# Mixture of softmaxes on one core: units in pairs through TensorE, and 4 MB stores

## The chip, the core and the metric

The kernel runs on one core of a Trainium2 chip. Its time is device time in microseconds from launch to end. The core's engines are TensorE (PE, matmuls into the accumulator memory PSUM), VectorE (DVE), ScalarE (ACT), GpSimd (POOL) and SyncE (SP), each with a queue of instructions worked off in order. 16 DMA engines move data between device memory and SBUF, the on-chip memory of 128 partitions; SP and ACT issue the DMAs here, and each has a queue of its own (q1 and q10 in the profile). A wait in an engine's queue holds everything behind it.

## What is computed

```
prior_probs = softmax(prior)                # (32, 128, 4): over the 4 heads
softmax     = softmax(logits)               # (32, 128, 4, 4096): over the vocabulary
out         = sum over the 4 heads of prior_probs * softmax   # (32, 128, 4096), fp32
```

268.4 MB of logits are read and 67.1 MB of output are written; a row of the vocabulary is 16 KB.

## The kernel before

The 4096 pairs of batch and position are cut into G = 32 groups of 128 rows, and each group into J = 2 units of M = 64 rows: N = 64 units. A unit's logits are 64 rows x 4 heads x 4096 values, 4 MB. They lie in one of SLOTS = 5 slots of 32 KB per partition: partition 2m + q holds heads 2q and 2q + 1 of row m, one behind the other (i = 0 and 1).

For each unit n and each i, `top` (L74) takes the negated maximum of 128 x 4096 values on DVE and then Exp on ACT, in place, with the sum in `dsum`. `weigh` (L83) takes the reciprocal on DVE, builds on POOL the 128 x 64 matrix `wt` (selection of the row, times 1/sum, times the prior's share) and issues eight matmuls of 512 columns: for c = 0 and 1, the column half c of the vocabulary goes to partitions 64c to 64c + 63 of the unit's accumulator. In the hardware each of these is two instructions, so that 16 stand in the profile for one pass. i = 0 starts the sums, i = 1 completes them. There are two accumulators of 128 x 2048 (four banks each), and a unit uses one of them, `accs[n % 2]`: unit n can be multiplied while unit n - 1 is evicted.

`evict` (L112) copies an accumulator on ACT to the group's home (L108): one half of `obuf`, `obuf[:, g % 2]`, so two groups alternate. As a partition holds only half of a row, `store` (L115) sends a group in two DMAs of 1 MB, each from 64 partitions, with 8 KB pieces. Both are issued on ACT's queue. The last groups are treated apart: units of groups 28 and 29 are put in slot 3, and stored after the loads (c = 0 on SP, c = 1 on ACT); groups 30 and 31 go out in parts as they are done.

The order of the work is written out by hand, and every engine keeps it. In turn n the kernel issues: `top(n, 0)`; `weigh(n - 1, 1)`, with the second pass of unit n - 1; on SP the load that reuses the slot of unit n - 1 (L165), which waits until PE has read it; `top(n, 1)`; `weigh(n, 0)`, with the first pass of unit n; `evict(n - 1)`; after every second unit the group's store.

Of the kernel before, what the change touches and what calls it, by code (L numbers as in the profile page):

```python
# [9 lines left out]
ALU = mybir.AluOpType  # L10
# [3 lines left out]
M = 64  # L14
J = 2
Q = 2
BANK = 512
SLOTS = 5


@with_exitstack
def kernel(
    ctx: ExitStack,
    tc: tile.TileContext,
    logits: bass.AP,
    prior: bass.AP,
    out: bass.AP,
):
    nc = tc.nc
    B, S, H, V = logits.shape  # L30
    R = M * J
    G = B * S // R
    N = G * J
    W = V // 2
    assert G * R == B * S and G == 32 and H == 2 * Q and V == 8 * BANK


    lg = logits.rearrange("b s h v -> (b s) h v").rearrange(
        "(g m j) (q i) v -> g j m q (i v)", m=M, j=J, i=Q
    )  # L40
    ov = out.rearrange("b s v -> (b s) v").rearrange("(g m j) v -> g m j v", m=M, j=J)
    pv = prior.rearrange("b s h -> (b s) h").rearrange("(g r) h -> g r h", r=R)

    cpool = ctx.enter_context(tc.tile_pool(name="cpool", bufs=1))
    psum = ctx.enter_context(tc.tile_pool(name="psum", bufs=1, space=bass.MemoryType.PSUM))

    slots = [cpool.tile([P, Q, V], FP32, name=f"slot{i}") for i in range(SLOTS)]

    obuf = cpool.tile([P, J, V], FP32, name="obuf")
    accs = [psum.tile([P, W], FP32, name=f"acc{i}") for i in range(2)]  # L50

    sel = cpool.tile([P, M], FP32, name="sel")
    wts = [[cpool.tile([P, M], FP32, name=f"wt{k}{i}") for i in range(Q)] for k in range(2)]
    pr = cpool.tile([G, R, H], FP32, name="pr")
    pn = cpool.tile([G, J, Q, M, Q], FP32, name="pn")
    pmax = cpool.tile([G, R], FP32, name="pmax")
    pp = cpool.tile([P, J, Q, G], FP32, name="pp")
    nmax = [cpool.tile([P, N], FP32, name=f"nmax{i}") for i in range(Q)]
    dsum = [cpool.tile([P, N], FP32, name=f"dsum{i}") for i in range(Q)]
    rden = [cpool.tile([P, N], FP32, name=f"rden{i}") for i in range(Q)]  # L60


    def slot(n):
        return slots[n % SLOTS if n < N - 6 else (4, 0, 1, 2)[(n - N + 6) % 4]]

    def load(n):
        src = lg[n // J, n % J]
        for i in range(0, Q, Q if n < N - 1 else 1):
            k = Q if n < N - 1 else 1
            nc.sync.dma_start(  # L70
                out=slot(n)[:, i : i + k], in_=src[:, :, i * V : (i + k) * V]
            )

    def top(n, i):  # L74
        x = slot(n)[:, i]
        nc.vector.tensor_reduce(  # L76
            out=nmax[i][:, n : n + 1], in_=x, axis=AX.X, op=ALU.max, negate=True
        )
        nc.scalar.activation(  # L79
            x, x, AF.Exp, bias=nmax[i][:, n : n + 1], accum_out=dsum[i][:, n : n + 1]  # L80
        )

    def weigh(n, i):  # L83
        nc.vector.reciprocal(rden[i][:, n : n + 1], dsum[i][:, n : n + 1])  # L84
        wt = wts[n % 2][i]
        nc.gpsimd.tensor_scalar(  # L86
            out=wt, in0=sel, scalar1=rden[i][:, n : n + 1],
            scalar2=pp[:, n % J, i, n // J : n // J + 1], op0=ALU.mult, op1=ALU.mult,
        )

        for b in range(W // BANK):
            for c in range(2):
                nc.tensor.matmul(  # L93
                    accs[n % 2][c * M : (c + 1) * M, b * BANK : (b + 1) * BANK],
                    lhsT=wt,
                    rhs=slot(n)[:, i, c * W + b * BANK : c * W + (b + 1) * BANK],
                    start=i == 0, stop=i == Q - 1,
                )

    def part(eng, g, c, js=slice(0, J), lo=0, hi=W):  # L100
        eng.dma_start(  # L101
            out=ov[g, :, js, c * W + lo : c * W + hi],
            in_=home(g)[c * M : (c + 1) * M, js, lo:hi],
        )

    HOLD = G - 4

    def home(g):  # L108
        x = slots[3] if HOLD <= g < G - 2 else obuf
        return x[:, g % 2].rearrange("p (j w) -> p j w", j=J)  # L110

    def evict(n, lo=0, hi=W):  # L112
        nc.scalar.copy(home(n // J)[:, n % J, lo:hi], accs[n % 2][:, lo:hi])  # L113

    def store(g):  # L115
        for c in range(2):
            part(nc.scalar, g, c)

    def prior_user(n):
        return max(k for k in range(n) if slot(k) is slot(n))  # L120

    with tc.manual_schedule():
        for n in range(SLOTS):
            load(n)
        nc.scalar.dma_start(out=pr, in_=pv)

        nc.gpsimd.memset(sel, 1.0)  # L127
        nc.gpsimd.affine_select(  # L128
            out=sel, in_=sel, compare_op=ALU.is_ge, fill=0.0, base=0,
            pattern=[[-Q, M]], channel_multiplier=1,  # L130
        )
        nc.gpsimd.affine_select(  # L132
            out=sel, in_=sel, compare_op=ALU.is_ge, fill=0.0, base=Q - 1,
            pattern=[[Q, M]], channel_multiplier=-1,
        )

        nc.vector.reduce_max(pmax, pr, axis=AX.X)  # L137
        nc.vector.tensor_sub(pr, pr, pmax.unsqueeze(2).to_broadcast([G, R, H]))  # L138
        nc.scalar.activation(pr, pr, AF.Exp)  # L139
        nc.vector.reduce_sum(pmax, pr, axis=AX.X)  # L140
        nc.vector.reciprocal(pmax, pmax)  # L141
        prv = pr.rearrange("g (m j) (q i) -> g j i m q", j=J, i=Q)
        pmv = pmax.rearrange("g (m j) -> g j m", j=J)
        for j in range(J):
            for i in range(Q):
                nc.vector.tensor_mul(  # L146
                    pn[:, j, i], prv[:, j, i], pmv[:, j].unsqueeze(2).to_broadcast([G, M, Q])
                )
        pq = pn.rearrange("g j i m q -> g j i (m q)")
        for t in range(P // 32):  # L150
            nc.vector.transpose(  # L151
                pp[32 * t : 32 * (t + 1)], pq[:, :, :, 32 * t : 32 * (t + 1)]
            )

        for n in range(N):
            w = n - 1
            top(n, 0)
            if n == N - 2:
                for g in (HOLD, HOLD + 1):
                    part(nc.scalar, g, 1)  # L160
            if w >= 0:
                weigh(w, 1)
                for k in range(SLOTS, N):
                    if prior_user(k) == w:
                        load(k)  # L165
                if w == N - 3:
                    for g in (HOLD, HOLD + 1):
                        part(nc.sync, g, 0)
            top(n, 1)
            weigh(n, 0)  # L170
            if w >= 0:
                evict(w)
                g = w // J
                if w % J == J - 1 and g < HOLD:
                    store(g)
                elif w == N - 3 or w == N - 2:
                    js = slice(0, J) if w == N - 3 else slice(0, 1)
                    part(nc.sync, g, 0, js)
                    part(nc.scalar, g, 1, js)

        n = N - 1
        weigh(n, 1)
        for lo in (0, W // 2):
            evict(n, lo, lo + W // 2)
            part(nc.sync, n // J, 0, slice(1, 2), lo, lo + W // 2)
            part(nc.scalar, n // J, 1, slice(1, 2), lo, lo + W // 2)
# [30 lines left out]
```

## Time and profile before

| | |
|---|---|
| median of three runs | 792.72 us (790.87 to 792.88) |
| the profiled execution: its time / its span | 793.28 / 791.6 us |
| busy: PE, DVE, ACT | 548.0, 573.3, 600.2 us (69%, 72%, 76%) |
| moved by DMA | 335.95 MB, mean 424 GB/s over the span |
| load of one unit | 4096 KB, 38.0 us from issue to landing (median) |
| store of half a group | 1024 KB, 21.5 us from issue to landing (median) |
| maximum / Exp / eviction, each | 4.41 / 3.71 / 1.82 us |

The time lies 1.7 us over the span, which runs from the first to the last instruction. Busy time is the sum of an engine's instructions. The time to landing of a DMA has its time in the queue in it. The page cuts the span into 40 slices and gives for each how busy an engine was, in tenths. A line number is a line of the kernel.

### The profile page before, as it was taken

Reading aid. Unit: us, or ns where it says so; the run is one execution under the profiler, and the core shown is the slowest. Engines: PE = TensorE matmul, PEld = TensorE weight load, DVE = VectorE, ACT = ScalarE, POOL = GpSimd, SP = SyncE. Lnnn points to the kernel's source line nnn. Section 1 sums busy time; section 2 is a strip of 40 time slices with the busy share of each in tenths; the row PEclk is TensorE's granted clock in tenths of the full one; section 3 lists DMA queues with packets and bytes.
Section 4 is the critical chain, followed back from the end, with each engine's and each line's share of the span. In section 5 each row is a group of like instructions: output and inputs, shape, how many; then the busy total and the mean of one; then the engine's idle time right before and its main releaser. Section 6 shows DMA issues by size and latency. Waiting matters only on the chain.

```text
span 791.6 us, 5426 instructions
## 1 busy us (share of the span) xinstructions
PE 548.0 (69%) x2048; PEld 160.4 (20%) x2048; DVE 573.3 (72%) x268; ACT 600.2 (76%) x323; POOL 51.6 (7%) x135
## 2 busy tenths in 40 slices
PE   0777568776687765767766767677578776687884
PEld 0222112221122221222211222222122221122221
DVE  5986867767768668677686676776867867768890
ACT  1897777787787787877877778778777787787894
POOL 0000000000000000000000000000000000000000
PEclk9999997899978899888999798789997799977897
DMA  9999999999999999999999999999999999999997
GB/s 376 442 416 431 431 428 430 432 431 427 434 432 435 429 432 436 430 433 431 434 429 433 431 431 429 428 435 431 429 431 432 431 432 433 433 430 436 429 416 229
DMA packets 18841, 335.95 MB, mean 424 GB/s; under 512 B 2144, under 2 KB 2144, under 8 KB 2432
## 3 DMA queue, kind: packets, MB, share of 16 engines
q1 hardware_dynamic: 10032, 272.63, 80.4%
q10 hardware_dynamic: 8784, 62.98, 19.1%
q8 instruction: 16, 0.26, 0.1%
q14 instruction: 9, 0.07, 0.0%
HBM read 268.50 MB, written 67.11 MB: 424 GB/s over the span
## 4 chain that ended last, share of the span: by engine, by line
DMA 73%; PE 12%; DVE 10%; ACT 2%; issue 1%; POOL 1%; ACTq 0%; SPq 0%; POOLq 0%
DMA slot<-in_logits_dram 73%; PE acc L93 12%; DVE nmax L76 10%; ACT slot L79 1%; POOL wt L86 1%; ACT obuf L113 1%; ACTq L101 0%; DVE rden L84 0%; SPq L70 0%; POOLq L86 0%; ACTq L79 0%; ACTq L113 0%
## 5 line engine op out<-in xcount | busy, mean ns | idle before, releaser
L93 PE MATMUL acc<-slot,wt 128*64 128x512 f32 x2048 | 548.0, 693 | 235.3 <-POOL wt L86 235.3
L76 DVE TENSOR_REDUCE nmax<-slot 128x1 f32<-128x4096 f32 x128 | 563.5, 4410 | 194.6 <-DMA slot<-in_logits_dram 194.6
L79 ACT ACTIVATE slot<-slot,nmax 128x4096 f32<-128x4096 f32 x128 | 474.6, 3708 | 178.0 <-DVE nmax L76 175.4
L93 PEld LDWEIGHTS acc<-slot,wt 128*64 128x64 f32 x2048 | 160.4, 158 | 622.0 <-POOL wt L86 311.8
L113 ACT COPY obuf<-acc 128x2048 f32<-128x2048 f32 (+1 forms) x61 | 110.9, 1817 | 4.8 <-PE acc L93 4.2
L86 POOL TENSOR_SCALAR wt<-sel,rden,pp 128x64 f32<-128x64 f32 x128 | 50.8, 397 | 725.7 <-DVE rden L84 721.8
L84 DVE RECIPROCAL rden<-dsum 128x1 f32<-128x1 f32 x128 | 19.6, 153 | 6.0 <-ACT slot L79 6.0
L79 ACT ACTIVATION_READ_ACCUMULATOR slot<-slot,nmax 128x1 f32 x128 | 23.9, 186 | 0.0
L113 ACT COPY slot<-acc 128x2048 f32<-128x2048 f32 x4 | 7.4, 1844 | 0.0
L137 DVE TENSOR_REDUCE pmax<-pr 32x128 f32<-32x512 f32 x1 | 0.7, 674 | 2.7 <-DMA pr<-in_prior_dram 2.7
L139 ACT ACT_TABLE_LOAD x1 | 1.3, 1283 | 1.2 <-PEq L201 1.2
L139 ACT ACTIVATE pr<-pr 32x512 f32<-32x512 f32 x1 | 0.6, 628 | 1.6 <-DVE pr L138 1.6
L151 DVE STREAM_TRANSPOSE pp<-pn 32x128 f32<-32x128 f32 x4 | 1.2, 302 | 0.1
L140 DVE TENSOR_REDUCE pmax<-pr 32x128 f32<-32x512 f32 x1 | 0.7, 674 | 0.7 <-ACT pr L139 0.7
L141 DVE RECIPROCAL pmax<-pmax 32x128 f32<-32x128 f32 x1 | 0.9, 942 | 0.0
L146 DVE TENSOR_TENSOR pn<-pr,pmax 32x128 f32<-32x128 f32 x4 | 0.9, 274 | 0.0
L138 DVE TENSOR_TENSOR pr<-pr,pmax 32x512 f32<-32x512 f32 x1 | 0.7, 678 | 0.0
L128 POOL TENSOR_SCALAR_AFFINE_SELECT sel<-sel 128x64 f32<-128x64 f32 x1 | 0.2, 241 | 0.1
L132 POOL TENSOR_SCALAR_AFFINE_SELECT sel<-sel 128x64 f32<-128x64 f32 x1 | 0.2, 240 | 0.1
L127 POOL MEMSET sel<- 128x64 f32 x1 | 0.2, 153 | 0.3 <-POOLq L201 0.3
L201 POOL MEMSET const-float32-0.0<- 128x1 f32 x1 | 0.1, 99 | 0.3 <-issue 0.3
L201 POOL MEMSET const-bfloat16-1.0<- 128x1 bf16 x1 | 0.1, 102 | 0.0
(2 smaller groups left out, 0.2 us busy)
## 6 DMA issues: line engine op xcount, KB each, us to landing
slot<-in_logits_dram SPq DMA_DIRECT2D x63, 4096.0 KB, 38.0
out_dram<-obuf ACTq DMA_DIRECT2D x57, 1024.0 KB, 21.5
slot<-in_logits_dram SPq DMA_DIRECT2D x2, 2048.0 KB, 20.2
out_dram<-slot SPq DMA_DIRECT2D x2, 1024.0 KB, 24.3
out_dram<-slot ACTq DMA_DIRECT2D x2, 1024.0 KB, 12.2
out_dram<-obuf SPq DMA_DIRECT2D x1, 1024.0 KB, 11.2
out_dram<-obuf SPq DMA_DIRECT2D x1, 512.0 KB, 4.3
out_dram<-obuf ACTq DMA_DIRECT2D x1, 512.0 KB, 6.2
```

The source lines that it names most:

```text
L76: nc.vector.tensor_reduce(out=nmax[i][:, n : n + 1], in_=x, axis=AX.X, op=ALU.max, negate=True)
L79: nc.scalar.activation(x, x, AF.Exp, bias=nmax[i][:, n : n + 1], accum_out=dsum[i][:, n : n + 1])
L84: nc.vector.reciprocal(rden[i][:, n : n + 1], dsum[i][:, n : n + 1])
L86: nc.gpsimd.tensor_scalar(out=wt, in0=sel, scalar1=rden[i][:, n : n + 1], scalar2=pp[:, n % J, i, n // J : n // J + 1], op0=ALU.mult, op1= ...
L93: nc.tensor.matmul(accs[n % 2][c * M : (c + 1) * M, b * BANK : (b + 1) * BANK], lhsT=wt, rhs=slot(n)[:, i, c * W + b * BANK : c * W + (b + ...
L113: nc.scalar.copy(home(n // J)[:, n % J, lo:hi], accs[n % 2][:, lo:hi])
L137: nc.vector.reduce_max(pmax, pr, axis=AX.X)
L138: nc.vector.tensor_sub(pr, pr, pmax.unsqueeze(2).to_broadcast([G, R, H]))
L139: nc.scalar.activation(pr, pr, AF.Exp)
L141: nc.vector.reciprocal(pmax, pmax)
L146: nc.vector.tensor_mul(pn[:, j, i], prv[:, j, i], pmv[:, j].unsqueeze(2).to_broadcast([G, M, Q]))
L151: nc.vector.transpose(pp[32 * t : 32 * (t + 1)], pq[:, :, :, 32 * t : 32 * (t + 1)])
```

## The change

Units are now taken through TensorE in pairs. Units 2k and 2k + 1 are the same half j of two neighbouring groups (`place`). In `pair_pass` the first one's rows go to partitions 0 to 63 and the second one's to partitions 64 to 127, each with its own weights, over the whole vocabulary: 16 matmuls (32 instructions) for one i, into both accumulators. A partition now holds a whole output row in the two accumulators. `pair_evict` copies both to `obuf[:, k % 2]`, and after two pairs a partition of `obuf` holds two neighbouring rows of the output, 32 KB in one piece. One DMA of 4 MB from all 128 partitions stores them: 32 KB pieces, on ACT's queue, after the eviction of every odd pair.

Units 0 to 55 are 28 pairs. The last eight units go singly, as before, with their results in slot 4 (groups 28 and 29) and in the slot of unit 60 (groups 30 and 31). The store of the last two pairs is issued on SP, behind the last load. The slots of a pair are reloaded together (`reload`), after the pair's second pass. The core of the diff:

```diff
+    TAIL = N - 8
+    def place(n):
+        if n < TAIL:
+            return 2 * (n // 4) + n % 2, n % 4 // 2
+        return n // J, n % J
     def slot(n):
-        return slots[n % SLOTS if n < N - 6 else (4, 0, 1, 2)[(n - N + 6) % 4]]
+        return slots[n % SLOTS if n < N - 5 else (n - N + 5) % 4]
...
+    def reload(n):
+        for k in range(SLOTS, N):
+            if max(x for x in range(k) if slot(x) is slot(k)) == n:
+                load(k)
...
+    def matmul(n, i, dst, lo):
+        nc.tensor.matmul(
+            dst, lhsT=wts[n % 2][i], rhs=slot(n)[:, i, lo : lo + BANK],
+            start=i == 0, stop=i == Q - 1,
+        )
+    def pair_pass(k, i):
+        for b in range(V // BANK):
+            for c in range(2):
+                acc = accs[b // 4][c * M : (c + 1) * M, b % 4 * BANK : (b % 4 + 1) * BANK]
+                matmul(2 * k + c, i, acc, b * BANK)
+    def pair_evict(k):
+        for h in range(2):
+            nc.scalar.copy(obuf[:, k % J, h * W : (h + 1) * W], accs[h])
+    def store(eng, k):
+        eng.dma_start(
+            out=ov[2 * k : 2 * k + 2].rearrange("g m j v -> (g m) j v"), in_=obuf
+        )
...
-    HOLD = G - 4
     def home(g):
-        x = slots[3] if HOLD <= g < G - 2 else obuf
+        x = slots[4] if g < G - 2 else slot(N - 4)
...
-        for n in range(N):
+        K = TAIL // 2
+        for k in range(K):
+            u, v = 2 * k, 2 * k + 1
+            top(u, 0)
+            if k:
+                weight(u - 1, 1)
+                pair_pass(k - 1, 1)
+                reload(u - 2)
+                reload(u - 1)
+            top(u, 1)
+            weight(u, 0)
+            if k:
+                pair_evict(k - 1)
+                if k % 2 == 0:
+                    store(nc.scalar, k // 2 - 1)
+            top(v, 0)
+            weight(u, 1)
+            top(v, 1)
+            weight(v, 0)
+            pair_pass(k, 0)
+
+        for n in range(TAIL, N):
...
+            if w == N - 3:
+                store(nc.sync, K // 2 - 1)
+                for g in (G - 4, G - 3):
+                    part(nc.sync, g, 0)
```

`weight` is the first half of the old `weigh`, without the matmuls; `unit_pass` is its second half, unchanged. In the loop over the last units `weight` and `unit_pass` stand where `weigh` stood, and in its first turn the second pass and the eviction of the last pair.

## The prediction

> **What bounds the kernel now.** I read the page first: slices, queues, chain, DMA issues.
>
> ```profile
> DMA  9999999999999999999999999999999999999997
> ...
> q1 hardware_dynamic: 10032, 272.63, 80.4%
> q10 hardware_dynamic: 8784, 62.98, 19.1%
> ...
> DMA 73%; PE 12%; DVE 10%; ACT 2%; issue 1%; POOL 1%; ACTq 0%; SPq 0%; POOLq 0%
> ...
> L113 ACT COPY obuf<-acc 128x2048 f32<-128x2048 f32 (+1 forms) x61 | 110.9, 1817 | 4.8 <-PE acc L93 4.2
> ```
>
> The 16 DMA engines are full from start to end, loads on q1 and stores on q10. The busiest engine, ACT, is at 76%. The evictions (L113) idled 4.8 us in all, and none of that for a store. To see what a load and a store cost, the timeline of DVE at the start, where no store runs yet:
>
> ```profile
> 23.29 4.42 DVE L76 TENSOR_REDUCE nmax<-slot 128x1 f32<-128x4096 f32 x1 [0.89 <-DMA slot<-in_logits_dram]
> 33.00 4.42 DVE L76 TENSOR_REDUCE nmax<-slot 128x1 f32<-128x4096 f32 x1 [0.84 <-DMA slot<-in_logits_dram]
> 42.71 4.42 DVE L76 TENSOR_REDUCE nmax<-slot 128x1 f32<-128x4096 f32 x1 [0.84 <-DMA slot<-in_logits_dram]
> ```
>
> A 4 MB load takes 9.71 us (432 GB/s). The timeline of PE much later shows the rhythm with stores:
>
> ```profile
> 607.14 8.78 PE L93 MATMUL acc<-slot,wt 128*64 128x512 f32 x32 [2.10 <-POOL wt L86]
> 619.25 9.85 PE L93 MATMUL acc<-slot,wt 128*64 128x512 f32 x32 [3.33 <-POOL wt L86]
> 631.36 8.78 PE L93 MATMUL acc<-slot,wt 128*64 128x512 f32 x32 [2.26 <-POOL wt L86]
> 643.47 3.65 PE L93 MATMUL acc<-slot,wt 128*64 128x512 f32 x16 [3.33 <-POOL wt L86]
> 647.86 3.65 PE L93 MATMUL acc<-slot,wt 128*64 128x512 f32 x16 [0.73 <-POOL wt L86]
> ```
>
> One unit each 12.11 us, so its 1 MB of stores costs 12.11 - 9.71 = 2.40 us. That is the load's rate already (9.71 / 4 = 2.43).
>
> **Larger store packets: 0 us.** Four units cost 4 x 12.11 = 48.4 us now, and 5 x 9.71 = 48.6 us as four loads and one 4 MB store. Loads and stores already move at one rate, so 32 KB packets have nothing to win. Bounds: by the whole-run queue shares q10's 62.98 MB took 2419 us of engine time (19.1% of 16 x 791.6) and would take 2352 at q1's rate, so at most 67 / 16 = 4 us are gained; the other way, 13 times 48.6 - 48.4, some 2 us are lost.
>
> **How the queues share.** The DMA view of 300 to 400 us, then that of the first store (issued at 47.42 into full load traffic):
>
> ```profile
> q1 hardware_dynamic: 1180, 34.47, 79.8%
> q10 hardware_dynamic: 1182, 8.63, 20.5%
> ```
>
> ```profile
> out_dram<-obuf ACTq DMA_DIRECT2D x1, 1024.0 KB, 17.5
> ```
>
> Packets of the two queues come one for one. A load packet is 32 KB, a store packet 8 KB now: stores get a fifth of the bytes and are spread evenly. With 32 KB packets a store takes half of the traffic while it lasts. The first store had 8 packets per engine, each beside one load packet: 8 x (9.71 + 2.40) / 8 = 12.1 us, so 17.5 - 12.1 = 5.4 us went before its first byte and after its last. The new 4 MB store has 8 packets per engine of a load packet's size: 2 x 9.71 + 5.4 = **24.8 us** from issue to landing. Bounds: with the fixed part of the 64 KB prior load on idle queues (1.9 us in all) 21.3; with a store that stands behind two whole queued loads, 44.
>
> [...]
>
> **What waits for that store.** Before, two groups' outputs alternate in obuf's halves. Now both halves are filled by two pairs and leave in one DMA, and the next pair_evict writes half 0: it must wait for the landing. On ACT the order is fixed: behind that eviction stands the Exp of the pair's second unit, behind it (by its sum) DVE's reciprocal, the POOL weight and both passes of the pair, and behind these the next eviction, the next store and, on SP, the reload of two slots at once.
>
> [...]
>
> **The loop, from one store issue to the next (four units):**
> - store to landing: 24.8
> - two evictions of 128x2048: 1.84 + 1.82 = 3.7 (ACT rows)
> - Exp with its accumulator read: 3.71 + 0.19 = 3.9
> - reciprocal, POOL weight, start of PE: 0.84 (773.61 to 774.45 in the timeline)
> - two pair passes of 32 matmuls: PE has idled about 11 us by then. After a gap 32 matmuls took 8.57 to 10.09 us, without one 2 x 3.55. I take 9.3 + 7.1 = 16.4; bounds 14.2 (both without a loss) and 20.2 (both at 10.09)
> - the last eviction half, then the issue: 1.9
>
> Sum **51.5 us**, against 48.6 that DMA needs: the loop is the bound, and the queues run dry for about 3 us each time round (from the last load of the five slots to the late reload). The other half of the loop is covered: from a store's issue over its 0.57 us on ACT, one Exp, 0.84, 16.4 and 1.9 the pair ends after 23.6 us, under the 28.5 of landing and evictions. DVE (573 us in all) and the reloads of the first pair end earlier too.
>
> **Start.** Units 0 to 4 land at 13.6, 23.3, 33.0, 42.7, 52.4. Pair 0's passes start at 33.0 and end at 49.4; its eviction at 51.3; Exp of unit 3 at 55.2; pair 1's passes at 56.0 to 72.4; the first store is issued at 74.3. The two reloads at 72.4 come about 2 us after the queue ran dry (unit 6 lands at 71.8, a load starts 1.5 us after its release).
>
> **End.** The 13th store is issued 12 loops later: 74.3 + 12 x 51.5 = 692.3. From there to the end of pair 27's passes 24.8 + 3.7 + 3.9 + 0.8 + 16.4 = 49.6, one eviction 1.9; then ACT has units 57 to 63 with 7 x 7.6 for Exp, 6 x 1.85 for evictions and 1.8 for issues: 66.1; then before's own end after the last Exp, 777.2 to 791.6 = 14.4. Together 132.0. The 4 MB of the last pair store, now behind the loads on SP, and 8 MB of parts take 29 us beside it: hidden. Span 692.3 + 132.0 = 824.3. The profiled execution took 793.28 for a span of 791.6, so 1.7 lie around it: **826 us**, against 793.28 (the median, 792.72, is 0.6 lower).
>
> The rest costs nothing: the new order of the units and the map of slots at the end change no size; matmuls, weight loads, Exp and reductions keep number and shape; 42 DMA issues less on ACT (0.57 each) give 24 us to an engine that then waits.
>
> **Rivals.**
> - **The store lands in time: faster.** If it lands within 21.5 us, the loop falls to about 48.2, below DMA's 48.6. For it: the prior load's 1.9 us. Against: the 17.5. Then 52.4 + 2 + (59 loads + 13 stores) x 9.71 = 753.5 to the last load, 12.6 MB at 432 GB/s 29, some 4 for the small parts and the landing: 786.5, so 788 us: the late stores fill an end in which the slice now has 229 GB/s. Deciding point: 21.9 us from issue to landing. Chance 0.13.
> - **Half of it.** Passes and landing near their lower ends, loop 48.7 to 49.8: 790 to 804 us. Chance 0.11.
> - **The columns no longer overlap**, because the two tiles now hold different weights and stream different slots: 32 matmuls take twice 7.1. Both halves of the loop grow to 37, the time to above 1100. Against: each matmul already has its own weight load (2048 of each). Chance 0.02. **The store stands behind queued loads** (44 us): loop 71, about 1070. Chance 0.04.
> - Forecast, loop 49.8 to 53: 804 to 845. Chance 0.70.
>
> **Numbers.** A microsecond in the loop is 12 to 13 in the time, hence the width: 792 to 846 leaves out the fast case, the far ones and little else (0.2). A measurement here can tell about 0.3% from no change: 790.3 to 795.1. The fast case lies below it (0.13); of "half of it" 0.04 lies in it; slower 0.83.
>
> **What would show it.** Right: ACT copies that idle some 6 to 7 us at every second pair with a DMA of out_dram as releaser, stores of 4096 KB landing 24 to 25 us after issue, DMA near 406 GB/s in the middle, equal packet counts while a store runs, PE bursts of 64 matmuls with 7 and 11 us between them. Wrong: copies that wait only for PE, slices at 430 GB/s, stores landing under 22 us, or 32 matmuls at 14 us.

## The result and the profile after

The changed kernel takes 833.98 us (median of four runs, 831.83 to 834.74) beside 792.8 of the kernel before: 1.0521 times as long [1.05, 1.0543]. The profiled execution took 834.57, with a span of 832.8. The forecast was 826, in a range of 792 to 846. One of the six executions of e7 (below) took 1916.78 us and is left out of e7's figures.

The GB/s row of the page of before, with 40 slices of the span:

```profile
GB/s 376 442 416 431 431 428 430 432 431 427 434 432 435 429 432 436 430 433 431 434 429 433 431 431 429 428 435 431 429 431 432 431 432 433 433 430 436 429 416 229
```

The page of the changed kernel: slices, queues, the group of the evictions, the stores.

```profile
DMA  9999999999999999999999999999999999999996
GB/s 381 428 427 379 434 396 403 429 386 443 383 428 427 376 430 380 422 428 384 430 380 444 430 381 429 369 435 433 373 430 378 430 408 401 430 379 427 413 342 230
...
q1 hardware_dynamic: 10176, 276.83, 80.2%
q10 hardware_dynamic: 2592, 58.79, 16.7%
...
L126 ACT COPY obuf<-acc 128x2048 f32<-128x2048 f32 x56 | 103.2, 1866 | 139.9 <-DMA out_dram<-obuf 104.1
...
out_dram<-obuf ACTq DMA_DIRECT2D x13, 4096.0 KB, 25.1
...
out_dram<-obuf SPq DMA_DIRECT2D x1, 4096.0 KB, 41.5
```

Read the DMA row and the row under it together. The tenths still say 9 everywhere. The GB/s row shows the loss: it swings between some 370 and 440, where before stays near 430, and the mean over the span is 403 where before had 424. The store's larger packets are there (q10 fell from 8784 to 2592 packets). The evictions, which idled 4.8 us in all before, now idle 139.9, and 104.1 of that for a store.

Where that wait stands is seen on ACT, in one loop from store issue to store issue. The columns are start, duration, engine, line, operation, and in brackets the idle time and its releaser:

```profile
73.71 0.37 ACTq L129 DMA_DIRECT2D out_dram<-obuf  x1
...
90.54 0.19 ACT L92 ACTIVATION_READ_ACCUMULATOR slot<-slot,nmax 128x1 f32 x1
99.22 3.63 ACT L126 COPY obuf<-acc 128x2048 f32<-128x2048 f32 x2 [8.49 <-DMA out_dram<-obuf]
102.73 3.72 ACT L92 ACTIVATE slot<-slot,nmax 128x4096 f32<-128x4096 f32 x1
...
123.56 1.86 ACT L126 COPY obuf<-acc 128x2048 f32<-128x2048 f32 x1 [1.57 <-PE acc L105]
125.46 0.34 ACTq L129 DMA_DIRECT2D out_dram<-obuf  x1
```

and on PE beside it:

```profile
101.18 1.94 PE L105 MATMUL acc<-slot,wt 128*64 128x512 f32 x2 [5.59 <-issue]
107.36 16.17 PE L105 MATMUL acc<-slot,wt 128*64 128x512 f32 x64 [4.24 <-POOL wt L99]
```

At 90.73 ACT has nothing left that it may do: next in its order are the copies, and they overwrite what the store of 73.71 still reads. They start at 99.22, 25.5 us after that store's issue. Exp and its accumulator read end at 106.54, the 64 matmuls run from 107.36 to 123.53, the last copy ends at 125.42, and the next store goes out. 25.5 + 3.5 + 3.8 + 0.8 + 16.2 + 1.9 is the loop of 51.7 us. Its mean over the twelve from 73.71 to 689.24 is 51.29.

The end, as windows (busy time of PE, PEld, DVE, ACT and POOL with their instructions, then granted clock, DMA share, GB/s):

```profile
780.00:800.00 20.00, 15.28 (x68) 4.23 (x64) 18.33 (x9) 18.55 (x11) 1.57 (x4) 1.00 1.00 390
800.00:810.00 10.00, 8.66 (x32) 2.55 (x32) 0.33 (x2) 5.94 (x5) 0.79 (x2) 0.83 0.99 305
810.00:820.00 10.00, 0.11 (x2) 0.00 (x0) 0.00 (x0) 2.02 (x2) 0.00 (x0) 0.75 1.01 376
820.00:832.80 12.80, 0.00 (x0) 0.00 (x0) 0.00 (x0) 0.00 (x0) 0.00 (x0) 0.50 0.46 137
```

The last load lands at 793.8 and the last Exp ends at 804.2, so that from 800 on little is left to compute and only stores are under way. The DMA engines show as full until 820, yet move 305 and 376 GB/s instead of the 432 of the loads.

### The profile page after: what moved, and what is told of

Read it like the earlier page. It is cut to its first block, busy times and chain, and to the rows that moved or that the text cites. A ratio compares the mean times of both kernels' runs of the same rounds, so it can differ in the third digit from the quotient of the medians.

```text
span 832.8 us, 5348 instructions
## 1 busy us (share of the span) xinstructions
PE 544.7 (65%) x2048; PEld 162.4 (20%) x2048; DVE 572.2 (69%) x268; ACT 600.2 (72%) x323; POOL 51.2 (6%) x135
## 3 DMA queue, kind: packets, MB, share of 16 engines
q10 hardware_dynamic: 2592, 58.79, 16.7%
## 5 line engine op out<-in xcount | busy, mean ns | idle before, releaser
L105 PE MATMUL acc<-slot,wt 128*64 128x512 f32 x2048 | 544.7, 675 | 265.4 <-POOL wt L99 196.1
L105 PEld LDWEIGHTS acc<-slot,wt 128*64 128x64 f32 x2048 | 162.4, 155 | 646.8 <-issue 402.7
L126 ACT COPY obuf<-acc 128x2048 f32<-128x2048 f32 x56 | 103.2, 1866 | 139.9 <-DMA out_dram<-obuf 104.1
L144 ACT COPY slot<-acc 128x2048 f32<-128x2048 f32 (+1 forms) x9 | 15.0, 1663 | 6.9 <-PE acc L105 4.2
## 6 DMA issues: line engine op xcount, KB each, us to landing
out_dram<-obuf ACTq DMA_DIRECT2D x13, 4096.0 KB, 25.1
out_dram<-obuf SPq DMA_DIRECT2D x1, 4096.0 KB, 41.5
out_dram<-slot ACTq DMA_DIRECT2D x1, 512.0 KB, 19.7
```

Of the source, the lines that this page charges most:

```text
L105: nc.tensor.matmul(dst, lhsT=wts[n % 2][i], rhs=slot(n)[:, i, lo : lo + BANK], start=i == 0, stop=i == Q - 1,)
L126: nc.scalar.copy(obuf[:, k % J, h * W : (h + 1) * W], accs[h])
```

## The experiments

The theories, with the letters used here. **S**: the eviction's wait for the store closes a loop (landing, eviction, Exp, passes, eviction, store) that is longer than the DMA work of four units. **P**: the pairing itself sets the pace. **Q**: a store that takes half of the traffic starves the loads. For the end, **W**: a late issue waits until an earlier DMA has landed (the ACT issue at 813.29 went out when the 41.5 us store had landed at 813.2); the expectations take it to be the DMA eight issues before. **N**: stores that read 64 partitions are slow when no loads run beside them.

### e1: smaller packets for the same store

`obuf`'s rows are set 64 bytes apart, so that its two rows no longer form one piece: 16 KB packets.

```diff
-    obuf = cpool.tile([P, J, V], FP32, name="obuf")
+    obuf = cpool.tile([P, J, V + 16], FP32, name="obuf")[:, :, :V]
```

> obuf's two rows stand 64 bytes apart, so the one 4 MB store goes out in 16 KB packets instead of 32 KB ones; nothing else changes. Theory S (the eviction that waits for the store's landing closes a loop through Exp, both passes, the next eviction and the next store): 16 store packets per engine, each beside a load packet, 16 x (1.214 + 0.607) + 5.4 = 34.5 us to landing instead of 25; the loop goes from the measured 51.3 to about 61, the time to about 950. Rival P (the pairing itself, with both accumulators taken and slots released by twos, sets the pace, and the store's wait is beside it): 834, no change. Rival Q (a store that takes half of the traffic starves the loads, and the time is lost there): it now takes a third, so faster, 805 to 820.

One run: 949.44 us.

```profile
L126 ACT COPY obuf<-acc 128x2048 f32<-128x2048 f32 x56 | 103.2, 1867 | 252.2 <-DMA out_dram<-obuf 217.8
...
out_dram<-obuf ACTq DMA_DIRECT2D x13, 4096.0 KB, 33.8
```

Landing goes from 25.1 to 33.8 us, 8.7 more; twelve loops of that are 104, and the time grew by 115. The loop itself went from 51.29 to 60.27 us, where some 61 were expected. A store that takes a smaller share of the traffic makes the kernel slower, which is the reverse of Q, and P knows nothing of packets. S holds.

### e2: the store cut in two

Each half of `obuf` has a DMA of its own (16 KB packets); the two are issued one behind the other, where the one was.

```diff
-        eng.dma_start(
-            out=ov[2 * k : 2 * k + 2].rearrange("g m j v -> (g m) j v"), in_=obuf
-        )
+        for j in range(J):
+            eng.dma_start(
+                out=ov[2 * k : 2 * k + 2, :, j].rearrange("g m v -> (g m) v"),
+                in_=obuf[:, j],
+            )
```

> The 4 MB store is issued at the same place as two DMAs of 2 MB, one for each half of obuf, so that the next pair's eviction waits for the first one's landing only. Bytes, packets (16 KB) and place are those of the padded kernel. Theory S: the first half lands after 8 x (1.214 + 0.607) + 5.4 = 20 us, the loop would be 46.5, under the 48.6 that DMA needs: 73.7 + 12 x 48.6 + an end of 143 + 1.7, about 801. Rival P: 834. Rival Q: the same as the padded kernel, 805 to 820 by its own count, since the traffic is the same.

799.64 us, 1.0097 times before [1.0079, 1.0114].

```profile
L126 ACT COPY obuf<-acc 128x2048 f32<-128x2048 f32 x56 | 102.9, 1860 | 30.6 <-PE acc L105 30.3
...
out_dram<-obuf ACTq DMA_DIRECT2D x26, 2048.0 KB, 24.4
```

The 24.4 is a median over both halves: the first ones land some 18.6 us after their issue (20 were expected), the second ones after some 30. A first half also goes out 2 to 4 us ahead of the second, while the copies into the second half still run, as the pair before has filled it. So it is free before the next copy asks for it, and no copy waits for a store. The loop takes 48.42 us, what DMA needs. The window of 300 to 600 us of before, of the changed kernel and of e2, in this order (the last figure is GB/s):

```profile
300.00:600.00 300.00, 209.95 (x780) 61.71 (x782) 219.21 (x100) 229.58 (x123) 19.83 (x50) 0.87 1.00 431
300.00:600.00 300.00, 201.35 (x736) 59.45 (x736) 208.30 (x96) 221.36 (x119) 18.48 (x47) 0.78 0.98 409
300.00:600.00 300.00, 210.40 (x804) 63.42 (x802) 221.15 (x99) 228.84 (x122) 19.26 (x49) 0.83 1.00 431
```

The rate is before's again. So 34.3 of the 41.2 us are the wait. The pairs, their order and the two slots reloaded at once are all still there.

### e3 and e10: an Exp ahead of the waiting eviction

In e3 `top(v, 0)` goes ahead of `pair_evict` in every turn; in e10 only for odd k, where the copies wait.

```diff
             weight(u, 0)
+            top(v, 0)
             if k:
...
-            top(v, 0)
```

> Maximum and Exp of the pair's second unit (first half) stand ahead of the previous pair's eviction instead of behind it; stores as in the changed kernel. Theory S: Exp, reciprocal and POOL leave the loop (4.7 us), 51.3 - 4.7 = 46.6, under DMA's 48.6: about 801, with stores that land 25 us after issue as now. Rival P: 834, as the pairs and the slots are handled as they were. Rival Q: 834, as the packets are the same.

e3: 809.0 us, 1.0204 times before [1.0166, 1.0242]. The copies wait 36.7 us for stores instead of 104.1, and the loop has 49.75 us instead of 51.29. The direction is S's, but 8 us of the expected gain are missing.

> Exp ahead of the eviction only in the pairs whose eviction waits for a store (odd k); in the others the eviction stays ahead, as in the changed kernel. Theory S with the reading of the run that moved Exp everywhere (there the other eviction, and so the next store, came to stand behind an Exp whose load was late): loop 25 + 1.9 + 16.4 + 1.9 = 45, under DMA's 48.6, about 798 to 802. If that reading is wrong: 806 to 811 again.

e10: 812.18 us, 1.0256 times before [1.0219, 1.0294]. A miss: my reading of e3 was wrong.

```profile
L126 ACT COPY obuf<-acc 128x2048 f32<-128x2048 f32 x56 | 101.9, 1854 | 4.3 <-PE acc L105 4.2
```

```profile
300.00:600.00 300.00, 203.93 (x776) 75.24 (x777) 213.31 (x97) 226.70 (x122) 18.87 (x48) 0.81 1.00 424
```

Now no copy waits for a store at all, and still the loops alternate between some 47.4 and 51.6 us, 49.58 in the mean, with the DMA engines full at 424 GB/s. The packet records show where it is: from 130 to 640 us a 32 KB load packet takes 1237 ns in the mean (1213 to 1215 in before and e2), and the slow ones come where the load queue is just running dry, because two slots are reloaded late and together (issues at 367.7 and 368.4). The store's larger packets are not needed for it: e1, with 16 KB store packets, has 1265 ns, and e4 (below), with no pair stores at all, 1256. Why a load packet is slow there no run takes apart; in e2 the two slots are reloaded together as well and nothing is lost. This part of e3 and e10 stays open.

### e4: no pair stores

The fourteen 4 MB stores are left out, everything else stays.

> The 14 stores of the pairs are left out (units 0 to 55 don't reach the output); evictions stay. Theory S: the pairs run at the rate of their own chain, Exp 3.9 + 0.84 + both passes 16.4 + the last eviction half 1.9 = 23.0 per pair, 46 per four units (loads alone need 38.8): 73.7 + 12 x 46 + an end of some 130, 755 to 765. Rival P (pairing alone costs the 51): 815 to 834. Rival Q (only the traffic counts): 38.8 per four units, some 665 to 690.

One run: 743.8 us. PE's timeline:

```profile
100.74 16.93 PE L105 MATMUL acc<-slot,wt 128*64 128x512 f32 x64 [6.47 <-POOL wt L99]
124.13 15.48 PE L105 MATMUL acc<-slot,wt 128*64 128x512 f32 x64 [6.47 <-POOL wt L99]
146.08 16.45 PE L105 MATMUL acc<-slot,wt 128*64 128x512 f32 x64 [6.47 <-POOL wt L99]
```

A pair every 22.75 us, 45.5 for four units. That is the pairing's own pace, and here it is the bound: the loads of four units need 38.8. It lies below the 48.4 us of four units with their stores, so P does not set the time of the changed kernel, with 3 us to spare in a loop. e4 is 11 us faster than S's lower end and some 13 under its sum: 6 of that are the twelve loops (45.5 against 46), and some 7 the end, which I had taken as 130 and which took 122.7.

### e5, e6 and e9: the end

In e5 the last unit is evicted and stored in one piece (two DMAs fewer, for W). In e6 and e9 each of the six 1 MB stores of groups 28 to 30 reads 128 partitions instead of 64, with as many bytes; e6 writes them as whole stretches, e9 to exactly the addresses of the changed kernel. In both the values of these three groups land in other places of the output than they should.

```diff
-        for lo in (0, W // 2):
-            evict(n, lo, lo + W // 2)
-            part(nc.sync, n // J, 0, slice(1, 2), lo, lo + W // 2)
-            part(nc.scalar, n // J, 1, slice(1, 2), lo, lo + W // 2)
+        evict(n)
+        part(nc.sync, n // J, 0, slice(1, 2))
+        part(nc.scalar, n // J, 1, slice(1, 2))
```

and in e9:

```diff
+        if js == slice(0, J):
+            rows = ov[g].rearrange("m j v -> (m j) v")
+            eng.dma_start(out=rows[:, c * W : (c + 1) * W], in_=home(g)[:, c])
+            return
```

> The changed kernel with the last unit's eviction and stores in one piece instead of two column halves: two DMAs less at the end. It asks why the end (from the 13th store's issue) took 143.6 us where 132.0 were forecast. Theory W (a DMA's issue waits until the DMA eight issues before it has landed, as the last four issues do in the trace, up to 822.8 us): the last issue comes at about 817, the time falls by 4 to 6 us, to 828 to 830. Theory N (with no loads beside them, stores from 64 partitions move at 300 to 390 GB/s instead of 432): bytes and shapes are the same, 832 to 834.

> The changed kernel with the six DMAs of 1 MB of groups 28, 29 and 30 reading all 128 partitions (half of each partition's bytes, 8 KB packets) instead of 64 partitions each: number, size, packets and places of issue stay; the rows of these three groups land in other places of the output. Theory N: 6.3 MB go at about 432 instead of some 345 GB/s, 3 to 5 us less, 829 to 831. Theory W: the waits stay, at most 1 us less, 833 to 834.

> As the run that took the six DMAs of 1 MB of groups 28 to 30 from 128 partitions, but each writes exactly the addresses that the changed kernel's DMA writes (128 rows, one column half, 8 KB pieces 16 KB apart, instead of 1 MB in one stretch); which value lands where is again not kept. If reading from 64 partitions is what slows stores without loads beside them: about 823, as that run. If it is the scattered destination: about 834, as the changed kernel.

e5: 832.56 us, 1.0503 times before [1.0483, 1.0523]: 1.4 us less than the changed kernel in the medians, with overlapping intervals. The last issue goes out at 816.8 instead of 822.8, as W had it, and the end hardly moves: the waits are in the trace, but are worth next to nothing.

e6: 823.3 us, 1.0394 times before [1.0381, 1.0408]; e9: 823.99, 1.0416 [1.0396, 1.0436]. Some 10 us less, more than twice what I had expected of N. e6's windows, from its last Exp on (it ends at 802.1):

```profile
800.00:810.00 10.00, 8.02 (x32) 2.40 (x28) 0.16 (x1) 5.21 (x5) 0.39 (x1) 0.86 1.01 425
810.00:821.80 11.80, 0.00 (x0) 0.00 (x0) 0.00 (x0) 0.65 (x1) 0.00 (x0) 0.63 0.75 276
```

425 GB/s stand where the changed kernel had 305 (e9 has 424). The packet records of the same 10 us show it too: an 8 KB packet on ACT's queue takes 515 ns in the mean in the changed kernel and 309 in e6 and e9. As e9 writes the same addresses, it is the reading of 64 partitions that is slow, not the pattern in device memory. N holds.

### e7, e8 and e11: both causes taken away

In e7 every pair has a 2 MB store of its own (the halves of `obuf` alternate). e8 is e7 with e5's edit. e11 is e7 with the 64-partition stores of groups 28 and 29 issued on ACT as soon as they are evicted, while loads still run, instead of after the loads.

```diff
+        g, j = 2 * (k // 2), k % J
         eng.dma_start(
-            out=ov[2 * k : 2 * k + 2].rearrange("g m j v -> (g m) j v"), in_=obuf
+            out=ov[g : g + 2, :, j].rearrange("g m v -> (g m) v"), in_=obuf[:, j]
         )
...
-                if k % 2 == 0:
-                    store(nc.scalar, k // 2 - 1)
+                if k - 1 < K - 2:
+                    store(nc.scalar, k - 1)
...
-                store(nc.sync, K // 2 - 1)
+                store(nc.sync, K - 2)
+                store(nc.sync, K - 1)
```

and in e11, beside e7's edit (the issues behind the loads are left out):

```diff
+            if n > TAIL and w % J and w < N - 4:
+                for c in range(2):
+                    part(nc.scalar, w // J, c)
```

> Every pair is stored by itself as soon as it is evicted: 2 MB from 128 partitions in 16 KB packets, the two halves of obuf alternating, so that a pair's eviction waits for the store of two pairs before. Theory S: landing in about 20 us of the 48.6 that lie between, no eviction waits for a store, DMA sets the pace; as the kernel with two DMAs, 796 to 801. A rival that is left, that the pairs' own chain (45.5 us per four units without stores) is late once stores stand beside it: above 805.

> The kernel that stores every pair by itself, with the last unit in one piece as well. By theory S and W together 4 to 6 us below the former, 792 to 796, about the time before the change (792.6); by N no different from the former.

> The kernel that stores every pair by itself, with groups 28 and 29 stored from ACT as soon as they are evicted, while loads still run, instead of behind the last load. If 64-partition stores are slow only without loads beside them: 4 MB fewer in the slow stretch, the last load 9.7 us later and the end 28.6 us behind it, 790 to 794, about the time before the change. If they cost the same anywhere: 797 to 800.

e7: 797.81 us, 1.0084 times before [1.0067, 1.0102]. e8: 798.39, 1.0078 [1.0065, 1.0091]: no change to e7, a second time against W. e11: 792.29, 1.0001 [0.9992, 1.001], as fast as before. e11's window of 300 to 600 us shows the full rate, with the pairs in place:

```profile
300.00:600.00 300.00, 210.78 (x800) 63.49 (x798) 220.27 (x100) 229.46 (x124) 19.47 (x50) 0.84 1.00 432
```

So the account nearly closes: the wait for the store is 34.3 us (after to e2), the late 64-partition stores 5.5 (e7 to e11), 39.8 of the 41.2 together. e2 and e7 differ by another 1.8, which no run takes apart. The 10.7 of e6 are not to be added: it gives six of the same stores other partitions, where e11 sends four of them earlier. No version that writes the whole output was faster than the kernel before.

## Why the prediction was right, and what was off

- **What bounds the kernel; larger packets bring 0.** Right. e11 has 16 KB packets where before has 8 KB, and moves 432 GB/s beside before's 431 in the same window. The 32 KB packets themselves: 1214 ns in the mean for one in the changed kernel, 4 x 310 = 1240 for as many bytes in before.
- **How the queues share.** Right: 24.8 us forecast, 25.1 measured. From 131 to 147 us, within one store, q10 moved 114 packets and q1 112 (16 of them tiny). e1 shows the packets of the two queues taking turns once more: with 16 KB pieces an engine has 16 to send for a store instead of 8, and the landing grows to 33.8 us (34.5 expected). Had an engine sent the pieces of a store without load packets between them, their size would not have mattered, as the bytes are the same.
- **What waits for that store.** Right: copies of every second pair, 13 waits, 8.0 us in the mean (forecast 6 to 7).
- **The loop.** Right: 51.5 forecast, 51.29 measured, term by term as in the timeline above. PE's burst is 16.2 (forecast 16.4). A detail that I had missed: two matmul instructions start before the burst, at 101.18, as the first accumulator has just been copied.
- **The queues run dry for 3 us each time round.** Right as a sum (51.29 - 48.4 = 2.9), partly wrong as a picture. The DMA share stays at 0.98 in the middle. A good part of the loss stands in the records as slower load packets, 1259 ns in the mean against 1213, which over 32 packets per engine and loop is 1.5 us.
- **Start.** The first store was forecast at 74.3 and went out at 73.7; the thirteenth at 692.3, and went out at 689.2.
- **End.** This is the term that was mis-sized: 132.0 forecast from the thirteenth store's issue to the end of the span, 143.6 measured, which is more than the 8 us by which the total was off (the earlier terms were 3 us too long). The step that failed is "The 4 MB of the last pair store, now behind the loads on SP, and 8 MB of parts take 29 us beside it: hidden". The computing in it was well sized: from the thirteenth store to the end of the last Exp 115.0, forecast 117.6. But after the last Exp 28.6 us followed, where I had taken before's 14.4. Two things are in it. When the last load had landed (793.8), 10.86 MB were still to be moved; at 432 GB/s these alone take 25 us, up to 819, about where before's 14.4 would have ended. So the stores had no room beside the computing and set the end. And they took 39 us, at a mean of 279 GB/s: stores that read 64 partitions with no loads beside them do not run at the load's rate. Giving 6 MB of them 128 partitions took 10.7 us off (e6) and left 19.7 after the last Exp (e9: 19.8). I had the sign in the page and passed over it: before's own last slice has 229 GB/s, and I had put that down to an end with little to move.
- **The rivals.** The deciding point of the fast one was a landing within 21.9 us; it was 25.1. e2 shows the case that it describes: with the wait gone the time falls to 799.64, not to that rival's 788, as the end keeps its slow stores. The columns overlap as before (2048 matmuls of 675 ns in the mean keep PE busy for 544.7 us; 693 ns and 548.0 us before), and the stores of the loop do not stand behind queued loads (25.1 us, not 44). The last one, put on SP behind the loads, does: 41.5 us to land.
- **What was put at nothing.** Right: ACT is busy for 600.2 us in both kernels, DVE and PE within 4 us of before. ACT issues 43 DMAs less, not 42.

Shown: the wait (e1, e2, e7), that pairing is not the bound (e4), and the 64-partition stores (e6, e9, e11). Not shown: why load packets are slow when the load queue runs dry, which goes with the loops of 49.6 to 49.8 us in e3 and e10.

## What to carry to other kernels

When a change joins two small transfers into a large one, ask first who overwrites its buffer next: the last user of the buffer, the landing of the transfer beside full traffic, and the work between form a loop, and its length decides; the packet size counted here only through the landing (e1: 33.8 us for 25.1, and a loop of 60.27 for 51.29). A store's time to landing beside the loads was found here from its packets per engine and the sizes of both queues' packets (24.8 us for 25.1; in e1 34.5 for 33.8; in e2 20 for 18.6); halving the transfer shortened the wait (18.6 us for the first half in e2), halving its packets alone lengthened it (33.8 in e1). Price the end of a kernel by the rows of its own end: the 432 GB/s that loads reach in the middle were not the rate of stores from half of the partitions at this end (305 GB/s from 800 to 810 us).

## What was not expected of the hardware

- **Stores from 64 partitions.** With no loads beside them (the last pair's store is still under way), they leave the DMA engines full by their share (0.99) at 305 GB/s; from 128 partitions 425 in the same place of the program. Beside loads they cost nothing that could be measured: e11, which issues four of them early, is 5.5 us faster than e7, and before, with 64-partition stores throughout, moves 431. Why 64 partitions are slower there no run takes apart.
- **The start of a store beside full queues.** In before, 5.4 us of the first store's 17.5 are not explained by its packets, and the same 5.4 gave the right landing for the 4 MB store (24.8 for 25.1). Most of it lies ahead of the first packet, which starts 4.4 us after the issue there and 4.9 in the changed kernel.
- **Slow packets after a gap.** 1237 to 1265 ns for a load packet in the mean of the kernels whose load queue runs dry now and then (the changed kernel, e1, e3, e4, e10), 1213 to 1215 in those where it does not (before, e2, e7, e11).
